# z weights ahead of the sums of blocks, low parts one sum behind, and a head's outputs sent from another tile, in a hybrid encoder layer on one Trainium2 core

## The chip, the cores and the metric

The kernel runs on one core of a Trainium2 chip. The metric is the device time of one execution in microseconds (us). Before the change the median of three runs is 2003.53 us.

## What is computed

One encoder layer over 1040 tokens (16 learned ones and 1024 of the input) of width 1024, all in float32. The part that matters here is the input projection and its users:

```python
proj = h @ w_in[l]
(q, k, v, z, b_raw, a_raw, sc_b, sc_c, sc_x, gate_a, gate_b) = jnp.split(proj, SPLIT_POINTS, axis=-1)
o_dn = gated_deltanet_bidir(q, k, v, z, b_raw, a_raw, conv_w, A_log, dt_bias, norm_w)  # ends in o * silu(z)
y_a = o_dn @ w_branch_dn[l]
y_b = (sc_b * depthwise_conv_centred(sc_c * sc_x, sc_conv_w[l])) @ w_branch_sc[l]
merged = jax.nn.sigmoid(gate_a) * y_a + jax.nn.sigmoid(gate_b) * y_b
h_res = h_res + merged @ w_out[l]
```

Then follow a SwiGLU block and a last normalisation. z has eight heads of 128 columns. gate_a and gate_b have eight column blocks of 128 each; block j of both is called pair j here.

## The kernel before

**Products in two parts.** A float32 operand is split into a high part, rounded to the type that TensorE (PE) takes in one pass, and a low part, the remainder: `split` (L100) lets ScalarE (ACT) copy the high part (L101) and VectorE (DVE) subtract it (L102). A product is then three matmuls per block of 128 rows: high by high, high by low, low by high. Weight blocks come by DMA into one of a few raw tiles and are split into tiles `wh` and `wl`, two slots each (`wtiles`, L111; `wload`, L117).

**Phase 1** (to about 970 us). Projections of all heads and of most other columns run on PE, and the scans of the eight heads lie between them, in an order that a planner writes out with estimated times. In `g_scan`, head h keeps its values in the tile `vS` (one buffer) and its decay matrices in `NP` (two buffers); the outputs replace parts of `NP`. At the end, for each half of the tokens, four transposes go to a bank, ACT copies the bank (L951) to a free part `oT` of `NP`, and a DMA stores it to `o_d[h]` (L953). The next head's values are written to `vS` by ACT (L808); the head after it writes `NP` by DVE (L639).

**The border** (from 970 us). The last three z-heads, 5, 6 and 7, and pairs 4 to 7 of the gates come after the scans. `z_rows(h)` runs z-head h in two halves of 24 matmuls (L134 to L136); ACT takes a tanh of the bank (L1493), DVE multiplies (L1495), and a DMA stores the result. The pairs use a scheme with seven block products in place of eight. It needs four sums of blocks of h, T1 to T4, each formed by DVE from large blocks (128x2048) and split in two parts. `moving_sums` (L1442) is a generator that forms one of them at each `next`: T1 in tiles mA, b3 and then b0; T2 in mA and b1; T3 in b3 and b2; T4 in mA and, after T3, b3. DVE's subtractions stand under L179, its additions under L1409, ACT's high parts under L101.

`pair(n, j, ...)` with n = j - 4 takes a bank of tag d (`pss`, three banks, in turn) and runs: A11 times B11 into it, ACT's copy of it (L1534), A12 times B21 into another bank, then S2 times T2 added into the first bank, S1 times T1, S3 times T3, S4 times B22 and A22 times T4, all at L1440. Pair 4's weights are prepared ahead, in three steps (`pair_weights`). z-head 7's two halves also use banks of tag d.

**What sets the order.** Phase 1 is written out for all engines. From L1484 to the end of pair 4, `border0` keeps DVE's and PE's instructions in the order of the code; ACT's and the queue's are placed by the scheduler, and so is all that comes after pair 4, which the scheduler may put between the instructions of the border. On each engine the built order is then fixed, and a waiting instruction holds those behind it.

Of the kernel before, what the change touches and what calls it, by code (L numbers as in the profile page):

```python
# [16 lines left out]
P = 128  # L17
# [7 lines left out]
H = 8  # L25
# [8 lines left out]
OQ, OK, OV, OZ, OBA, OSB, OSC, OSX, OGA, OGB = (  # L34
    0, 1024, 2048, 3072, 4096, 4128, 5152, 6176, 7200, 8224)


def unit(col):

    return (col if col < OBA else col - 32) // P  # L40
# [8 lines left out]
def encoder_layer(ctx: ExitStack, tc: tile.TileContext, x, meta, norm1_w, w_in, w_ba,  # L49
                  dn_conv_w, A_log, dt_bias, dn_norm_w, sc_conv_w, w_bdn, w_bsc,  # L50
                  w_out, norm2_w, w_gu, w_down, final_w, out):
    nc = tc.nc
# [12 lines left out]
    def uid(s):  # L65
        cnt["n"] += 1
        return f"{s}_{cnt['n']}"
# [29 lines left out]
    def transpose(dst, src, n=P):  # L97
        nc.tensor.transpose(dst, src, ident[:n, :n])

    def split(hi, lo, src):  # L100
        nc.scalar.copy(hi, src)  # L101
        nc.vector.tensor_tensor(out=lo, in0=src, in1=hi.bitcast(F32), op=ALU.subtract)  # L102
# [8 lines left out]
    def wtiles(shape):  # L111
        return [wp.tile(shape, F32R, tag=g, name=uid(g), bufs=2) for g in ("wh", "wl")]

    def staged(shape):
        return *wtiles(shape), rawtile(shape)

    def wload(src, j):  # L117
        wh, wl, raw = staged([P, KT, P])
        nc.sync.dma_start(raw, src[j])
        split(wh, wl, raw)  # L120
        return wh, wl
# [56 lines left out]
    def sub(out, a, b):  # L178
        nc.vector.tensor_tensor(out=out, in0=a, in1=b, op=ALU.subtract)  # L179
# [91 lines left out]
    def pe(ns):  # L271
        T["pe"] += ns
        return T["pe"] + HOP

    def V(n, kind=0):
        return on("dve", (68 + 1.042 * n, 130 + 1.042 * n, 130 + 0.52 * n)[kind])

    def A(n):
        return on("act", 144 + 0.834 * n)
# [505 lines left out]
    def g_scan(h, st_):  # L785
        nonlocal freed
        kq, vT, small, kn, NP, PQ, Pm = (st_[k] for k in ("kq", "vT", "small", "kn", "NP", "PQ", "Pm"))
# [4 lines left out]
        vS = dn.tile([P, 9, P], F32, tag="vS", name=uid("vS"))  # L792
        yield from take("scan")

        def newbank():
            return pss().rearrange("p (a n) -> p a n", a=4)
# [63 lines left out]
        for i in range(NC):  # L860
# [6 lines left out]
            t = pe(215 * len(act_))  # L867
# [5 lines left out]
            for d in act_:  # L873
# [4 lines left out]
                t = V(P, 1)  # L878
# [7 lines left out]
            for d in range(2):  # L886
# [3 lines left out]
                t = A(P)  # L890
# [5 lines left out]
            if i < NC - 1:  # L896
# [3 lines left out]
                t = pe(430)  # L900
# [3 lines left out]
            t2 = pe(430)  # L904
            if i < NC - 1:
                yield t
                for d in range(2):
# [6 lines left out]
                    t = V(P, 1)  # L914
# [28 lines left out]
            yield T["pe"] + 300  # L943
        yield T["dve"] + HOP
        for c4 in range(2):
            oT = NP[:, 4 * c4:4 * c4 + 4, 1 - c4]
            pt = newbank()
            for c in range(4):
                transpose(pt[:, c], oacc[4 * c4 + c])
            yield pe(430)  # L950
            nc.scalar.copy(oT, pt)  # L951
            A(512)
            nc.sync.dma_start(o_d[h][:, c4 * 512:(c4 + 1) * 512].rearrange("p (c t) -> p c t", c=4), oT)  # L953
# [82 lines left out]
    with tc.tile_pool(name="st", bufs=1) as st:  # L1036
# [64 lines left out]
        def high(t, g):  # L1101
            p = size(t)
            nc.scalar.copy(hx[0][:, 4 * g:4 * g + 4, C0 + P * t:C0 + P * t + p], banks[t, g][:, :, :p])  # L1103
# [297 lines left out]
    def big(tag, shape, dtype=F32R):  # L1401
        return tp.tile(shape, dtype, tag=tag, name=uid(tag))
# [9 lines left out]
    mov = {}  # L1412
# [29 lines left out]
    def moving_sums():  # L1442

        c = [slice(C0 + META + 512 * i, C0 + META + 512 * i + 512) for i in range(2)]
        f = lambda m: m.bitcast(F32)
        h0, h1 = ([f(hx[0][:, 4 * i:4 * i + 4, cc]) for cc in c] for i in range(2))
        l0, l1, l2 = ([f(t[:, :, cc]) for cc in c] for t in low_tiles)
        for i in range(2):
            for j in range(2):
                mov[f"B{i + 1}{j + 1}"] = hx[0][:, 4 * i:4 * i + 4, c[j]], [hx[1][4 * i + k][:, c[j]] for k in range(4)]  # L1450
        for i, n in enumerate(("T1", "T2", "T3")):
            t = big(f"b{i}", [P, 2, 4, 512])
            mov[n] = t[:, 0], t[:, 1]
        x, y = (big(g, [P, 2, 4, 512], F32) for g in ("mA", "b3"))
        t1, t2, t3, d_ = x[:, 0], x[:, 1], y[:, 0], y[:, 1]
        a, b = slice(0, 2), slice(2, 4)
        sub(t1, h0[1], h0[0])
        sub(d_, l0[1], l0[0])
        add(t1, t1, d_)
        split(*mov["T1"], t1)  # L1460
        yield
        sub(t2, h1[1], t1)
        add(t2[:, a], t2[:, a], l1[1])
        add(t2[:, b], t2[:, b], l2[1])
        split(*mov["T2"], t2)
        yield
        sub(t3, h1[1], h0[1])
        sub(d_[:, a], l1[1], l0[1][:, a])
        sub(d_[:, b], l2[1], l0[1][:, b])
        add(t3, t3, d_)  # L1470
        split(*mov["T3"], t3)
        yield
        t = big("b3", [P, 2, 4, 512])
        mov["T4"] = t[:, 0], t[:, 1]
        sub(t1, h1[0], t2)
        add(t1[:, a], t1[:, a], l1[0])
        add(t1[:, b], t1[:, b], l2[0])
        split(*mov["T4"], t1)
        yield

    raw_slots.extend((tp, f"raw{i}") for i in range(2))
    left, right = slice(0, 512), slice(512, 1024)
    border0 = ExitStack()
    border0.enter_context(tc.manual_schedule(engines={mybir.EngineType.DVE, mybir.EngineType.PE}))  # L1484
    z_units = [wload(w_in, unit(OZ + ZH * P))]

    def z_rows(h):
# [13 lines left out]
    def pair_weights(n, j):  # L1501

        s_hl[n % 2] = big(("mB", "mA")[n % 2], [P, 2, 2, KT, P])
        if n == 0:
            u = big("w2", [P, 2, 4, P])
            u_hl[0] = u[:, 0], u[:, 1]
        elif n == 1:
            u_hl[1] = [tp.tile([P, 4, P], F32R, tag="t2", name=uid("u_hl"), bufs=2) for _ in range(2)]
        gh, gl = wtiles([P, KT, P])
        rg, ru = (rawtile([P, KT, P]) for _ in range(2))  # L1510
        nc.sync.dma_start(rg, w_in[unit(OGA + j * P)])
        nc.sync.dma_start(ru, w_in[unit(OGB + j * P)])
        A_ = {"A11": (gh[:, 0:4], gl[:, 0:4]), "A12": (gh[:, 4:8], gl[:, 4:8])}

        def first():
            split(gh, gl, rg)

        def second():
            split(*u_hl[n % 2], ru[:, 4:8])
            A_["A22"] = u_hl[n % 2]  # L1520
            sums(rg, ru, rg[:, 0:4], rg[:, 4:8], ru[:, 0:4], ru[:, 4:8])
            stationary2(n, ru, rg, ru, A_)
        return A_, first, second

    def pair(n, j, A_, first, second):
# [54 lines left out]
        return o1  # L1580

    sums_of_blocks = moving_sums()
    z0, z1, z2 = (z_rows(h) for h in range(ZH, H))
    next(sums_of_blocks)
    z_units.append(wload(w_in, unit(OZ + (ZH + 1) * P)))
    next(z0)
    next(z0)
    next(sums_of_blocks)
    z_units.append(wload(w_in, unit(OZ + (H - 1) * P)))
    next(z0)  # L1590
    pair0 = pair_weights(0, GH)
    next(z1)
    pair0[1]()
    next(z1)
    pair0[2]()
    next(z1)
    next(z2)
    next(sums_of_blocks)
    next(z2)
    next(sums_of_blocks)  # L1600
    next(z2)
    for n, j in enumerate(range(GH, KT)):
        o1 = pair(n, j, *(pair_weights(n, j) if n else pair0))
        if n == 0:
            border0.close()
# [55 lines left out]
    mov = {n: (b_hl[:, 2 * i], b_hl[:, 2 * i + 1]) for i, n in enumerate(("B11", "B21"))}  # L1661
# [84 lines left out]
    t = KT - 1  # L1746
# [229 lines left out]
```

## Time and profile before

| | |
|---|---|
| runs | 2002.02, 2003.53, 2005.52 us |
| the profiled execution | 2004.27 us |
| its span, first to last instruction | 2002.5 us |
| PE busy | 1977.3 us, 99% of the span |
| DVE, ACT busy | 1396.6 us, 836.4 us |
| mean granted clock of PE | 0.995 |
| border, z-heads 5 to 7 on PE | 970.18 to 1009.33 us |

The profile is of one execution; what lies around its span is 2004.27 - 2002.5 = 1.77 us. Rows of a list in order of time read: start, duration, engine, line, operation, output <- inputs (names of tiles without numbers), shapes, and in brackets the idle time of the engine before it with what ended it. "pm", "pe" and "pd" are banks of the tags m, e and d. A table of stretches gives each engine's busy time with the number of its instructions, PE's granted clock (1.00 is full speed) and the DMA's share.

### The profile page before, as it was taken

To read this page: it belongs to the slowest core of one execution; us is meant where nothing else is said; L and a number is where in the kernel's file an instruction comes from. 1 tells how busy PE (TensorE), PEld (TensorE's weight loads), DVE (VectorE), ACT (ScalarE), POOL (GpSimd) and SP (SyncE) were. 2 spreads that over 40 slices of the span, in tenths; PEclk is the share of its full clock that TensorE was granted. 3 is DMA by queue.
4 is the path that set the end of the run, shared out by engine and by line. 5 is a ranking of instruction groups with operands and counts; after the bars stand their busy time and mean duration, and the time that the engine had idled before them with its cause. 6 is when DMAs were issued, how large, how long until landed. Compare 5 with 4: busy or idle time off the path is not lost.

```text
span 2002.5 us, 31873 instructions
## 1 busy us (share of the span) xinstructions
PE 1977.3 (99%) x12011; PEld 1724.1 (86%) x12011; DVE 1396.6 (70%) x3013; ACT 836.4 (42%) x1961; POOL 107.8 (5%) x407
## 2 busy tenths in 40 slices
PE   9999999999999999999999999999999999999998
PEld 8998889899999999999788888887878888888887
DVE  6887688878888888855685544469766666656575
ACT  6472465536463646333244221225323333334344
POOL 2011101010101010100000000000000000000000
PEclk9999999999999999999999999999999999999999
DMA  3123222222132222221236743123765345477654
GB/s 132 65 90 95 80 80 75 85 61 83 45 99 59 75 59 75 59 65 43 95 116 242 249 160 95 63 93 110 256 217 217 123 155 188 158 273 244 195 172 167
DMA packets 131121, 251.00 MB, mean 125 GB/s; under 512 B 45013, under 2 KB 54662, under 8 KB 128535
## 3 DMA queue, kind: packets, MB, share of 16 engines
q1 hardware_dynamic: 130391, 247.92, 37.5%
q8 instruction: 94, 1.54, 0.3%
q10 hardware_dynamic: 576, 1.05, 0.1%
q14 instruction: 60, 0.49, 0.1%
HBM read 180.67 MB, written 68.25 MB: 124 GB/s over the span
## 4 chain that ended last, share of the span: by engine, by line
PE 90%; DVE 4%; DMA 3%; ACT 1%; issue 1%; SPq 0%; DVEq 0%; ACTq 0%
PE pm L341 33%; PE pd L1440 12%; PE pe L1440 5%; PE pm L1440 3%; PE pd L903 1%; PE pd L882 1%; PE pd L866 1%; PE pe L136 1%; PE pe L134 1%; PE pd L869 1%; PE pe L135 1%; PE pe L603 1%; PE pd L134 1%; PE pd L136 1%; PE pd L135 1%; PE pe L1882 1%
## 5 line engine op out<-in xcount | busy, mean ns | idle before, releaser
L341 PE MATMUL pm<-hTh,wh 128*128 128x512 f32 (+4 forms) x1296 | 446.4, 350 | 0.3 <-ACT hTh L1103 0.2
L341 PE MATMUL pm<-al,wh 128*128 128x512 f32 (+4 forms) x1296 | 445.9, 349 | 0.0
L341 PE MATMUL pm<-hTh,wl 128*128 128x512 f32 (+4 forms) x1296 | 443.8, 348 | 0.0
L341 PEld LDWEIGHTS pm<-hTh,wh 128*128 128x128 f32 x1296 | 242.7, 188 | 13.7 <-issue 0.8
L341 PEld LDWEIGHTS pm<-hTh,wl 128*128 128x128 f32 x1296 | 242.9, 188 | 12.3 <-issue 0.4
L341 PEld LDWEIGHTS pm<-al,wh 128*128 128x128 f32 x1296 | 242.9, 188 | 12.2 <-issue 0.4
L102 DVE TENSOR_TENSOR al<-raw,ring_h 128x1024 fp32r<-128x1024 f32 x73 | 88.6, 1222 | 65.0 <-ACT ring_h L101 64.7
L101 ACT CAST ring_h<-raw 128x1024 fp32r<-128x1024 f32 x73 | 76.7, 1053 | 107.8 <-PE pd L1884 34.4
L990 DVE TENSOR_TENSOR wl<-raw,wh 128x512 fp32r<-128x512 f32 x118 | 79.5, 688 | 30.6 <-ACT wh L993 30.2
L363 DVE SCALAR_TENSOR_TENSOR kq<-ra,wc,kq 128x520 f32<-128x520 f32 x128 | 96.6, 755 | 4.8 <-ACT kq L393 3.5
L889 ACT ACTIVATE w<-pd,small 128x128 f32<-128x128 f32 x128 | 39.9, 363 | 117.1 <-PE pd L882 116.7
L101 ACT CAST wh<-raw 128x1024 fp32r<-128x1024 f32 x47 | 49.3, 1050 | 87.4 <-PE pe L135 25.5
L496 DVE TENSOR_TENSOR tm<-fP,fN 128x135 f32<-128x135 f32 (+23 forms) x248 | 72.0, 290 | 4.9
L500 DVE TENSOR_TENSOR fP<-fP,tm 128x135 f32<-128x135 f32 (+23 forms) x248 | 71.6, 289 | 5.1
L993 ACT CAST wh<-raw 128x512 fp32r<-128x512 f32 x118 | 69.2, 621 | 3.7 <-issue 3.6
L1409 DVE TENSOR_TENSOR b<-pd,b 128x512 f32<-128x512 f32 x22 | 15.2, 690 | 69.4 <-PE pd L1440 69.4
L1819 ACT ACTIVATE b<-b 128x512 f32<-128x512 f32 x22 | 13.9, 632 | 114.3 <-DVE b L1409 114.3
L102 DVE TENSOR_TENSOR wl<-raw,wh 128x1024 fp32r<-128x1024 f32 x47 | 57.3, 1219 | 3.8 <-ACT wh L101 3.7
L856 ACT ACTIVATE jk<-NP 128x128 f32<-128x128 f32 x64 | 19.9, 311 | 83.5 <-DVE NP L852 82.5
L876 DVE SCALAR_TENSOR_TENSOR r<-pd,negEG,vS 128x128 f32<-128x128 f32 x120 | 36.8, 345 | 25.7 <-PE pd L866 25.2
L1440 PE MATMUL pd<-b_hl,wh 128*128 128x512 f32 x176 | 54.5, 391 | 0.0
L912 DVE SCALAR_TENSOR_TENSOR S<-S,eGl,pd 128x128 f32<-128x128 f32 x104 | 31.6, 342 | 30.2 <-PE pd L899 29.8
(590 smaller groups left out, 4689.5 us busy)
## 6 DMA issues: line engine op xcount, KB each, us to landing
raw<-in_w_in_dram SPq DMA_DIRECT2D x72, 512.0 KB
raw<-in_w_gate_up_dram SPq DMA_DIRECT2D x44, 512.0 KB
sums<-in_w_down_dram SPq DMA_DIRECT2D x22, 512.0 KB
t_d<-sums SPq DMA_DIRECT2D x11, 1024.0 KB
raw<-s_d SPq DMA_DIRECT2D x44, 256.0 KB
raw<-t_d SPq DMA_DIRECT2D x44, 256.0 KB
act_d<-b SPq DMA_DIRECT2D x43, 256.0 KB
raw<-act_d SPq DMA_DIRECT2D x33, 256.0 KB
```

Source lines behind the costliest of these rows:

```text
L101: nc.scalar.copy(hi, src)
L102: nc.vector.tensor_tensor(out=lo, in0=src, in1=hi.bitcast(F32), op=ALU.subtract)
L134: mm(po[:m, :n], wh[:, k, :m], xhk[:, t0:t0 + n], start=(k == 0), stop=False)
L135: mm(po[:m, :n], wh[:, k, :m], xlk[:, t0:t0 + n], start=False, stop=False)
L136: mm(po[:m, :n], wl[:, k, :m], xhk[:, t0:t0 + n], start=False, stop=(k == KT - 1))
L341: mm(po[:, :n], ww[:, k], f(k)[:, t0:t0 + n], start=i == 0, stop=i == 3 * KT - 1)
L363: nc.vector.scalar_tensor_tensor(out=acc, in0=raw[:, h0 + t:h0 + t + hn], scalar=wc[:, t, col:col + 1], in1=acc, op0=ALU.mult, op1=ALU.add)
L496: nc.vector.tensor_tensor(out=tv, in0=fP[:, 0:r, j:j + 1].broadcast_to([P, r, n]), in1=fN[:, j:j + 1, j + 1:32].broadcast_to([P, r, n]), o ...
L500: nc.vector.tensor_tensor(out=fP[:, 0:r, j + 1:32], in0=fP[:, 0:r, j + 1:32], in1=tv, op=ALU.subtract)
L990: nc.vector.tensor_tensor(out=u[1][1][:, k], in0=u[2][:, k], in1=u[1][0][:, k].bitcast(F32), op=ALU.subtract)
L993: nc.scalar.copy(u[1][0][:, k], u[2][:, k])
L1440: mm(po, x[:, k], y, start=k + i == 0 and not add_to, stop=k == 3 and i == 2, skip_group_check=add_to)
```

## The change

The outputs of a head go by way of `vS` in place of `NP`. `moving_sums` gives out a high part in one step and its low part in the next, with the next sum's DVE work between them, so that it has more steps. z-head 6's weights are loaded and split ahead of T1, z-head 7's after T2's high part. ACT joins DVE and PE in `border0`.

```diff
@@ g_scan
-            oT = NP[:, 4 * c4:4 * c4 + 4, 1 - c4]
+            oT = vS[:, 4 * c4:4 * c4 + 4]
@@ moving_sums
+        high = lambda n, t: nc.scalar.copy(mov[n][0], t)
+        low_part = lambda n, t: sub(mov[n][1], t, f(mov[n][0]))
         sub(t1, h0[1], h0[0])
         sub(d_, l0[1], l0[0])
         add(t1, t1, d_)
-        split(*mov["T1"], t1)
+        high("T1", t1)
         yield
         sub(t2, h1[1], t1)
         add(t2[:, a], t2[:, a], l1[1])
         add(t2[:, b], t2[:, b], l2[1])
-        split(*mov["T2"], t2)
+        high("T2", t2)
+        low_part("T1", t1)
+        yield
+        low_part("T2", t2)
         yield
         sub(t3, h1[1], h0[1])
         sub(d_[:, a], l1[1], l0[1][:, a])
         sub(d_[:, b], l2[1], l0[1][:, b])
         add(t3, t3, d_)
-        split(*mov["T3"], t3)
+        high("T3", t3)
+        yield
+        sub(t1, h1[0], t2)
+        low_part("T3", t3)
         yield
         t = big("b3", [P, 2, 4, 512])
         mov["T4"] = t[:, 0], t[:, 1]
-        sub(t1, h1[0], t2)
         add(t1[:, a], t1[:, a], l1[0])
         add(t1[:, b], t1[:, b], l2[0])
-        split(*mov["T4"], t1)
+        high("T4", t1)
+        yield
+        low_part("T4", t1)
         yield
@@ the border
-    border0.enter_context(tc.manual_schedule(engines={mybir.EngineType.DVE, mybir.EngineType.PE}))
+    border0.enter_context(tc.manual_schedule(engines={mybir.EngineType.DVE, mybir.EngineType.PE, mybir.EngineType.Activation}))
...
-    next(sums_of_blocks)
     z_units.append(wload(w_in, unit(OZ + (ZH + 1) * P)))
     next(z0)
+    next(sums_of_blocks)
+    next(sums_of_blocks)
     next(z0)
+    z_units.append(wload(w_in, unit(OZ + (H - 1) * P)))
     next(sums_of_blocks)
-    z_units.append(wload(w_in, unit(OZ + (H - 1) * P)))
     next(z0)
+    next(z1)
     pair0 = pair_weights(0, GH)
     next(z1)
     pair0[1]()
     next(z1)
     pair0[2]()
-    next(z1)
     next(z2)
     next(sums_of_blocks)
     next(z2)
     next(sums_of_blocks)
+    next(sums_of_blocks)
     next(z2)
+    next(sums_of_blocks)
```

In the built order tile names carry numbers that differ between the two programs. DVE at the start of the border, before the change (wl_12346 is the low part of z-head 6's weights, b_2088_12335 T1's low part):

```order
L179 TENSOR_TENSOR mA_12338<-hTh 128x2048
L179 TENSOR_TENSOR b_2092_12339<-al_124 128x2048
L1409 TENSOR_TENSOR mA_12338<-mA_12338,b_2092_12339 128x2048
L102 TENSOR_TENSOR b_2088_12335<-mA_12338,b_2088_12335 128x2048
L102 TENSOR_TENSOR wl_12346<-raw_12347,wh_12345 128x1024
```

The same place now (wl_12336 is z-head 6's, b_2093_12368 T1's low part):

```order
L102 TENSOR_TENSOR wl_12336<-raw_12337,wh_12335 128x1024
L179 TENSOR_TENSOR mA_12371<-hTh 128x2048
L179 TENSOR_TENSOR b_2097_12372<-al_124 128x2048
L1409 TENSOR_TENSOR mA_12371<-mA_12371,b_2097_12372 128x2048
L179 TENSOR_TENSOR mA_12371<-hTh,mA_12371 128x2048
L1409 TENSOR_TENSOR mA_12371<-mA_12371,al_125 128x1024
L1409 TENSOR_TENSOR mA_12371<-mA_12371,al_126 128x1024
L179 TENSOR_TENSOR b_2093_12368<-mA_12371,b_2093_12368 128x2048
```

The weights have moved ahead of T1, and T1's low part behind the forming of T2.

PE after pair 4's second product, before the change (pm_12578 is that product's bank, pd_12564 pair 4's bank of tag d, mB_12418 holds its S blocks, b_2089_12336 is T2; twelve matmuls each):

```order
L1440 MATMUL pm_12578<-al_126,wh_12420 128x512
L1440 MATMUL pm_12578<-hTh,wl_12421 128x512
L1440 MATMUL pd_12564<-b_2089_12336,mB_12418 128x512 x12
L1440 MATMUL pe_12593<-b_2088_12335,mB_12418 128x512 x12
L1440 MATMUL pd_12564<-b_2090_12337,mB_12418 128x512
```

The same place now. pd_12675 is pair 5's bank and pd_12795 pair 6's; pair 5's three rows shown are the last of twelve matmuls, A11 times B11:

```order
L1440 MATMUL pm_12578<-al_126,wh_12447 128x512
L1440 MATMUL pm_12578<-hTh,wl_12448 128x512
...
L1440 MATMUL pd_12675<-hTh,wh_12667 128x512
L1440 MATMUL pd_12675<-al_124,wh_12667 128x512
L1440 MATMUL pd_12675<-hTh,wl_12668 128x512
L1440 MATMUL pd_12795<-hTh,wh_12787 128x512
L1440 MATMUL pd_12795<-al_124,wh_12787 128x512
L1440 MATMUL pd_12564<-b_2094_12369,mB_12445 128x512 x12
L1440 MATMUL pe_12593<-b_2093_12368,mB_12445 128x512 x12
```

Fourteen matmuls of pairs 5 and 6 now stand ahead of pair 4's third product. In the order before the change, pair 5's twelve come behind pair 4's S4 times B22.

DVE now, from pair 4's last S block to the operation on z-head 7's second half (pd_12495 and pd_12527 are the banks of z-head 7's halves; b_2097_12372 is where T3 is formed, mA_12371 T4, b_2095_12370 T3's low part):

```order
L102 TENSOR_TENSOR mB_12445<-raw_12450,mB_12445 128x1024
L179 TENSOR_TENSOR b_2097_12372<-hTh 128x2048
L179 TENSOR_TENSOR b_2097_12372<-al_125,al_124 128x1024
L179 TENSOR_TENSOR b_2097_12372<-al_126,al_124 128x1024
L102 TENSOR_TENSOR wl_12668<-raw_12669,wh_12667 128x1024
L1409 TENSOR_TENSOR b_2097_12372<-b_2097_12372 128x2048
L1504 TENSOR_SCALAR s_2111_12494<-s_2111_12494,pd_12495 128x512
L179 TENSOR_TENSOR mA_12371<-hTh,mA_12371 128x2048
L179 TENSOR_TENSOR b_2095_12370<-b_2097_12372,b_2095_12370 128x2048
L1409 TENSOR_TENSOR mA_12371<-mA_12371,al_125 128x1024
L1409 TENSOR_TENSOR mA_12371<-mA_12371,al_126 128x1024
L1504 TENSOR_SCALAR s_2111_12494<-s_2111_12494,pd_12527 128x512
```

Before, the order was T3's forming, T3's low part, the operation on the first half, T4's forming, T4's low part, the operation on the second half. T3's low part has moved behind the first operation, into the forming of T4, and T4's low part behind the second. On ACT the copy of pair 4's bank (L1534, now L1543) stood directly behind the tanh of z-head 7's second half; now it is here (b_2114_12555 is T4's high part):

```order
L1457 COPY b_2095_12370<-b_2097_12372 128x2048
L1502 ACTIVATE s_2111_12494<-pd_12527 128x512
L1457 COPY b_2114_12555<-mA_12371 128x2048
L1543 COPY s_2115_12562<-pd_12564 128x512
```

T4's high part now stands ahead of that copy.

## The prediction

> **What bounds the kernel now.** I read the page first, for the shares of the engines and the chain that ended last; then the idle time of PE with its releasers; then, around the one stall that the diff touches, the instructions of DVE, ACT and PE in order of time, and a table of short stretches with the granted clock.
>
> ```profile
> PE 1977.3 (99%) x12011; PEld 1724.1 (86%) x12011; DVE 1396.6 (70%) x3013; ACT 836.4 (42%) x1961; POOL 107.8 (5%) x407
> PE 90%; DVE 4%; DMA 3%; ACT 1%; issue 1%; SPq 0%; DVEq 0%; ACTq 0%
> ```
>
> PE is busy 99% of the span and carries 90% of the chain. A change that leaves PE's work as it is can only take away PE's idle time, or its time at a low clock, or add to them. The work is untouched here: every matmul of before is in the changed program.
>
> ```profile
> 970.18 0.39 PE L134 MATMUL pm<-hTh,wh 128*128 128x512 f32 x1
> ...
> 981.29 0.39 PE L135 MATMUL pe<-al,wh 128*128 128x512 f32 x1
> 985.51 0.79 PE L136 MATMUL pe<-hTh,wl 128*128 128x512 f32 x1 [3.83 <-DVE wl L102]
> ...
> 998.45 0.39 PE L134 MATMUL pd<-hTh,wh 128*128 128x512 f32 x1
> ...
> 1014.77 2.88 PE L1440 MATMUL pd<-b,mB 128*128 128x512 f32 x12
> ...
> 1028.14 0.39 PE L1440 MATMUL pd<-hTh,wh 128*128 128x512 f32 x1
> ```
>
> These are PE's rows at the border between the heads' phase and the pairs. The z-heads 5, 6 and 7 run from 970.18, 48 matmuls each. The 50th matmul starts at 981.29, so one takes (981.29 - 970.18) / 49 = 0.2267 us. The third matmul of z-head 6 then waits 3.83 us for DVE's low part of its weights. At 1014.77 pair 4 starts its third product, S2 times T2.
>
> ```profile
> core 0: us, PE busy (x) PEld busy (x) DVE busy (x) ACT busy (x) POOL busy (x), PEclk, DMA share, GB/s
> 981.70:985.50 3.80, 0.00 (x0) 0.00 (x0) 3.47 (x3) 1.72 (x3) 0.00 (x0) 0.78 0.00 0
> 985.50:990.60 5.10, 5.09 (x12) 4.03 (x13) 5.07 (x4) 0.00 (x0) 0.00 (x0) 0.50 0.31 103
> 990.60:1000.00 9.40, 9.40 (x42) 7.79 (x42) 4.52 (x5) 4.04 (x4) 0.00 (x0) 1.00 0.29 81
> 1492.60:1494.60 2.00, 0.02 (x1) 0.00 (x0) 1.97 (x4) 0.00 (x0) 0.00 (x0) 1.00 0.00 0
> 1495.80:1499.20 3.40, 3.40 (x10) 2.66 (x9) 0.69 (x1) 0.40 (x2) 0.00 (x0) 0.50 0.78 284
> ```
>
> The stall costs more than its 3.83 us: the clock is 0.50 until 990.60, and 12 matmuls take 5.10 us there, 0.425 us each. Even an idle time of 2.0 us, at 1492.60, was followed by 3.4 us at 0.50.
>
> **Term A, the stall that goes.** Why was the low part late?
>
> ```profile
> 970.15 1.05 ACT L101 CAST wh<-raw 128x1024 fp32r<-128x1024 f32 x1 [9.82 <-PE pm L341]
> 980.09 1.91 ACT L101 CAST b<-mA 128x2048 fp32r<-128x2048 f32 x1 [3.67 <-DVE mA L1409]
> 998.47 1.05 ACT L101 CAST wh<-raw 128x1024 fp32r<-128x1024 f32 x1 [4.66 <-PE pe L135]
> 999.42 0.58 ACT L1493 ACTIVATE s<-pe 128x512 f32<-128x512 f32 x1
> 1012.25 0.59 ACT L1534 COPY s<-pd 128x512 f32<-128x512 f32 x1 [1.36 <-PE pd L1440]
> ```
>
> ```profile
> 970.38 0.69 DVE L451 TENSOR_TENSOR rb<-pm,rb 128x512 f32<-128x512 f32 x1 [4.70 <-PE pm L341]
> 973.24 2.29 DVE L179 TENSOR_TENSOR mA<-hTh 128x2048 f32<-128x2048 f32 x1 [2.16 <-DMA p_d<-rb]
> 975.45 2.28 DVE L179 TENSOR_TENSOR b<-al 128x2048 f32<-128x2048 f32 x1
> 977.76 2.29 DVE L1409 TENSOR_TENSOR mA<-mA,b 128x2048 f32<-128x2048 f32 x1
> 982.03 2.29 DVE L102 TENSOR_TENSOR b<-mA,b 128x2048 fp32r<-128x2048 f32 x1 [1.98 <-ACT b L101]
> 984.24 1.22 DVE L102 TENSOR_TENSOR wl<-raw,wh 128x1024 fp32r<-128x1024 f32 x1
> ...
> 999.55 1.23 DVE L102 TENSOR_TENSOR wl<-raw,wh 128x1024 fp32r<-128x1024 f32 x1 [2.90 <-ACT wh L101]
> ...
> 1007.43 2.36 DVE L102 TENSOR_TENSOR mB<-raw,mB 128x1024 fp32r<-128x1024 f32 x2 [1.12 <-ACT mB L101]
> 1009.71 0.68 DVE L1495 SCALAR_TENSOR_TENSOR s<-s,pe 128x512 f32<-128x512 f32 x1
> 1010.31 2.28 DVE L179 TENSOR_TENSOR b<-hTh 128x2048 f32<-128x2048 f32 x1
> ...
> 1015.91 2.28 DVE L1409 TENSOR_TENSOR b<-b 128x2048 f32<-128x2048 f32 x1
> ...
> 1022.66 0.68 DVE L1495 SCALAR_TENSOR_TENSOR s<-s,pd 128x512 f32<-128x512 f32 x1
> 1023.26 2.28 DVE L179 TENSOR_TENSOR mA<-hTh,mA 128x2048 f32<-128x2048 f32 x1
> 1025.58 2.36 DVE L1409 TENSOR_TENSOR mA<-mA,al 128x1024 f32<-128x1024 f32 x2
> ```
>
> The high part of z-head 6's weights was there at 970.15 + 1.05 = 971.2, but the low part stood on DVE behind all of T1, and T1's low part waited for ACT. Now it stands in front: DVE is free at 971.07, so it is done at 971.2 + 1.22 = 972.4, before T1 can start (973.24, when the transfer out of the memory under mA has ended), and 9 us before PE asks for it. The cover is those 9 us. So A = -(3.83 + 12 x (0.425 - 0.2267)) = **-6.2 us**.
>
> Z-head 7's weights take the slot of z-head 5, free at 970.18 + 48 x 0.2267 = 981.06. ACT now does both high parts first. T1 ends on DVE at 980.05, T2's subtraction and two additions (2.28 + 2.36) end about 984.6, T2's high part at 986.5, a tanh and the cast (0.58 + 1.05) at 988.1, and after 1.22 us of DVE the low part at 989.4. PE asks at 970.18 + 98 x 0.2267 = 992.4. That is hidden with 3 us to spare, and T1's and T2's low parts (2.29 each) lie beside z-heads 6 and 7.
>
> **Term B, what is late next.** Without the stall PE ends z-head 6 at 970.18 + 96 x 0.2267 = 991.94, z-head 7 at 1002.83, and pair 4's first two products at 1008.27. By then both parts of T2 are ready, but pair 4's third product is no longer next in PE's queue: the built order puts twelve matmuls of pair 5's first product and two of pair 6's in front of it. Banks of tag d are three, taken in turn: z-head 7's two halves and pair 4 hold them, so pair 5's request gets the bank of z-head 7's first half and pair 6's that of its second. DVE's operation on that half (L1495, now L1504) must have read it first. DVE has that operation behind the forming of T3, and the one on the second half behind T3's low part and the forming of T4. In before, pair 5's product started at 1028.14, after the operation of 1022.66: no wait. PE does not pass a waiting matmul (at 981.29 the matmuls behind the waiting one had their data, and none ran).
>
> When does DVE get there? Pair 4's weights need z-head 6's slot, so DVE's chain hangs on the end of z-head 6. In before, from that end (998.45) to T3's first operation (1010.31) it took 11.86 us. The chain now has one operation of 0.60 us less on DVE, and one tanh of 0.58 us more ahead of it on ACT: 991.94 + 11.86 = 1003.8. T3's formation takes 1015.91 + 2.28 - 1010.31 = 7.88 us, the operation on the bank 0.6 more: **1012.3**. PE idles 4.0 us. Then T4's subtraction, T3's low part, two additions and the operation on the second half: 2.28 + 2.29 + 2.36 + 0.68, less 0.3 for starts that overlap (973.24 to 975.45 is 2.21), 7.3 us: **1019.6**. Pair 5's twelve matmuls are long done by then, at either clock.
>
> Next comes the third product, which adds to pair 4's bank and so waits for ACT's copy of it (L1534, now L1543). With ACT's order now written out too, that copy stands behind T4's high part. In before the copy ran at 1012.25, 16 us ahead of T4. T4's high part starts when the additions are done, about 1019.0, takes 1.91, and the copy 0.59: **1021.5**.
>
> So from 1008.27 to 1021.5, 13.2 us, PE issues 14 matmuls, worth 14 x 0.2267 = 3.2 us. B = **+10.1 us**. Behind the two waiting products stands all of PE's work; nothing of it gets through.
>
> **Term C, the clock.** No row shows this pattern of idle times (4.0, then 2 to 5, then 1.5 us, with 14 matmuls between). Nearest are the 5.10 us (12 matmuls, 2.4 us lost) and the 3.4 us after 1495.80. Bounds: 0, if the clock is back when the third product starts, and 2.4. I take one stretch of 3.4 us at half speed, 8 matmuls at 0.425: 8 x 0.2 = **+1.6 us**, as the last idle time before it is the short one.
>
> The Trainium skill ("TensorE: Matmul & The Clock Gate", section "Why this matters for your kernels") says that PE gaps up to about 3 us keep the clock, and that an idle window of about 3.4 us halves it. The trace disagrees: 2.0 us sufficed at 1492.60. By the page the short idle times at the end would cost nothing and C would be 0.
>
> **Term D, the heads' outputs.** The copy and the two transfers keep their place in all queues, only the tile differs. What it moves are two waits for the transfer.
>
> ```profile
> 375.80 0.38 SPq L953 DMA_DIRECT2D o_d<-NP  x1
> 382.64 0.61 DVE L639 SCALAR_TENSOR_TENSOR NP<-pe,small,PQ 128x128 f32<-128x128 f32 x2 [1.41 <-DMA o_d<-NP]
> 883.07 1.28 SPq L953 DMA_DIRECT2D o_d<-NP  x2
> 892.85 0.86 ACT L808 ACTIVATE vS<-pd,small 16x128 f32<-16x128 f32 x3 [1.50 <-PE pd L98]
> ```
>
> Once NP was held 1.41 us by a transfer that landed 6.8 us after its issue; that wait goes, though PE shows no idle time there. In its place the next head's values wait for the same transfer, as vS has one buffer. The shortest distance is the last head's, 884.35 to 892.85, 8.5 us, against 6.8 us for the slowest landing: covered by 1.7 us. I take 0, with -1.4 and +1 as ends; the scan behind ACT would pay if the cover went.
>
> **Sum.** The profiled execution took 2004.27 us (span 2002.5, and 1.77 around it): 2004.27 - 6.2 + 10.1 + 1.6 = **2009.8 us**. The median shown is 2003.53, 0.7 below, within the spread of the three runs (2002.02 to 2005.52). Past pair 4 the orders soon agree again and DVE and ACT have slack, so I let the shift stand to the end.
>
> **Rivals.**
> 1. Faster: the stall goes and nothing takes its place, 2004.27 - 6.2 = 1998.1. It needs DVE and ACT to reach pair 4's copy early. The full gain needs the copy done by 1008.27 + 3.2 = 1011.4; the point of no change is 1014.77 + 14 x 0.2267 = 1017.9, where before had issued as many matmuls. For it: DVE's chain holds idle times of 2.90 and 1.12 us. Against: the first was mostly PE's own work on z-head 6, and without both the copy still ends at 1017.5. Chance 0.05.
> 2. The clock is full again at the third product (the page's rule, and the lower end of C): 2008.2. For it, 14 matmuls run between the waits; against, 2.0 us of idleness was enough. Chance 0.14.
> 3. The edits give a little back, D's 1.4 us and 1 to 2 us of DVE's idle times: 2005 to 2007.5. Chance 0.09.
> 4. The low clock lasts for two stretches, or DVE's backlog stops PE once more within pair 4: 2011.8 to 2013. T4's low part ends near 1024 and is needed at 1032, which speaks against. Chance 0.08.
>
> That the edit doesn't do what it says is excluded by the built order: the weights do stand in front. My forecast, 2008.5 to 2011.5, has 0.64.
>
> **How the numbers follow.** A measurement of this kernel tells about 0.2% from no change, 4.0 us: 1999.5 to 2007.5. Faster is rival 1, 0.05. Within is rival 3 and the low edge of rival 2, 0.11. Slower is the rest, 0.84. The range leaves out rival 1, part of rival 3 and the upper half of rival 4: 2006.5 to 2012.6.
>
> **What would show it.** Right, if PE has no idle time before 1008, z-head 6 ends near 992, and then three idle times follow: about 4 us before pair 5's first product, released by DVE's operation on z-head 7; 2 to 5 us before pair 6's two matmuls, by the same line; and 1 to 2 us before S2 times T2, by ACT's copy; with a clock of 0.5 around them. T3's first operation should start near 1004 and the copy end near 1021.5. Wrong, if pair 5's product starts by 1010, if the copy on ACT runs before T4's high part, or if vS waits for a DMA.

## The result, and the profile after

The changed kernel takes **2009.22 us**, median of 8 runs (2006.81 to 2010.51). The kernel before takes 2003.55 us beside it, median of 8 runs (2001.18 to 2006.41). The ratio is 1.0028, 95% interval 1.0019 to 1.0037: slower by 0.28%. The profiled execution took 2007.99 us, with a span of 2006.3 us.

From the page after, the engines' busy time and the shares of the chain that ended last:

```profile
PE 1978.7 (99%) x12011; PEld 1724.6 (86%) x12011; DVE 1396.7 (70%) x3013; ACT 836.3 (42%) x1961; POOL 107.4 (5%) x407
PE 89%; DVE 5%; DMA 2%; ACT 2%; issue 1%; SPq 0%; DVEq 0%; ACTq 0%
```

The counts of instructions are those of before. PE's share of the chain is down from 90% to 89% and DVE's up from 4% to 5%: a per cent is 20 us, too coarse for this difference, so the rows at the border have to tell.

PE's rows at the border after, in order of time (start, duration, instruction; in brackets the idle time ahead of it and what released it):

```profile
1002.68 0.39 PE L1440 MATMUL pd<-hTh,wh 128*128 128x512 f32 x1
...
1007.89 0.39 PE L1440 MATMUL pm<-hTh,wl 128*128 128x512 f32 x1
1012.36 0.77 PE L1440 MATMUL pd<-hTh,wh 128*128 128x512 f32 x1 [4.08 <-DVE s L1504]
...
1017.19 0.63 PE L1440 MATMUL pd<-hTh,wl 128*128 128x512 f32 x1
1019.54 0.50 PE L1440 MATMUL pd<-hTh,wh 128*128 128x512 f32 x1 [1.72 <-DVE s L1504]
1019.88 0.40 PE L1440 MATMUL pd<-al,wh 128*128 128x512 f32 x1
1021.47 4.47 PE L1440 MATMUL pd<-b,mB 128*128 128x512 f32 x12 [1.18 <-issue]
1025.78 2.89 PE L1440 MATMUL pe<-b,mB 128*128 128x512 f32 x12
```

The 3.83 us stall of z-head 6 is gone, and pair 4 starts at 1002.68 where it would have with no idle time at all. But pair 4's third product, S2 times T2, starts at 1021.47. In before it started at 1014.77. Three new idle times stand in front of it: 4.08 us, released by DVE's operation on the first bank of z-head 7; 1.72 us, by the same line for the second bank; and 1.18 us for which the profile names nothing. The rows of DVE and ACT name it:

```profile
1003.72 2.28 DVE L179 TENSOR_TENSOR b<-hTh 128x2048 f32<-128x2048 f32 x1
...
1011.53 0.68 DVE L1504 SCALAR_TENSOR_TENSOR s<-s,pd 128x512 f32<-128x512 f32 x1
...
1018.81 0.68 DVE L1504 SCALAR_TENSOR_TENSOR s<-s,pd 128x512 f32<-128x512 f32 x1
```

```profile
992.00 0.60 ACT L1502 ACTIVATE s<-pe 128x512 f32<-128x512 f32 x1 [3.49 <-PE pe L136]
...
1011.65 1.90 ACT L1457 CAST b<-b 128x2048 fp32r<-128x2048 f32 x1 [2.47 <-DVE b L1409]
...
1018.98 1.91 ACT L1457 CAST b<-mA 128x2048 fp32r<-128x2048 f32 x1 [4.93 <-DVE mA L1409]
1020.79 0.57 ACT L1543 COPY s<-pd 128x512 f32<-128x512 f32 x1
```

ACT idles 4.93 us ahead of T4's high part (1018.98), and pair 4's copy stands behind it although the copy's data have been there since pair 4's first product, that is since about 1005.6. The copy ends at 1020.79 + 0.57 = 1021.36, and S2 times T2 starts 0.11 us later.

A table of short stretches of after, cut where the granted clock changes and each 3.41 us long, shows the clock (busy time and number of instructions of each engine, then the granted clock):

```profile
core 0: us, PE busy (x) PEld busy (x) DVE busy (x) ACT busy (x) POOL busy (x), PEclk, DMA share, GB/s
1010.96:1014.38 3.42, 2.02 (x5) 1.66 (x6) 3.42 (x4) 2.40 (x2) 0.00 (x0) 0.50 0.00 0
1014.38:1017.79 3.41, 3.41 (x9) 2.14 (x7) 3.41 (x4) 0.00 (x0) 0.00 (x0) 0.50 0.00 0
1017.79:1021.20 3.41, 0.77 (x3) 0.30 (x2) 3.41 (x5) 2.22 (x2) 0.00 (x0) 1.00 0.26 105
1021.20:1024.61 3.41, 3.14 (x8) 2.50 (x9) 3.41 (x5) 1.31 (x3) 0.00 (x0) 0.50 0.14 54
```

The clock is at 0.50 from 1010.96 to 1017.79 and from 1021.20 to 1024.61. The first of the two costs nothing: it slows the twelve matmuls of pair 5, which end before the second bank is free. The second slows S2 times T2: 1025.78 - 1021.47 = 4.31 us for twelve matmuls instead of 2.72.

**Where the time went.** S2 times T2 starts 1021.47 - 1014.77 = 6.7 us later than before, with 14 matmuls (3.2 us) already done that came behind it in before: +3.5 us. The low clock in it adds 4.31 - 2.72 = 1.6, together +5.1 us at the border. The profiled executions differ by less in the end, 2007.99 - 2004.27 = 3.7 us. Far behind the border, near 1385 us, the same matmul starts 4.8 us later than in before (1390.09 against 1385.32), 0.3 less than this sum; a low clock that lasts longer there adds 0.9. Then one stall gives more than that back, first in before, then in after:

```profile
1494.67 4.55 PE L1440 MATMUL pd<-b,w 128*128 128x512 f32 x12 [2.05 <-DVE b L1409]
```

```profile
1500.19 3.02 PE L1440 MATMUL pd<-b,w 128*128 128x512 f32 x12 [1.75 <-DVE b L1409]
```

The idle time ahead of it is 0.3 us shorter after, and the twelve matmuls behind it ran at full clock, 3.02 us instead of 4.55: 1.8 us won back. These are single executions; the medians of 8 runs each differ by 5.7 us.

### The profile page after: what moved, and what is told of

Its sections match the earlier page's. It is cut to its first block, busy times and chain, and to the rows that moved or that the text cites. A ratio compares the mean times of both kernels' runs of the same rounds, so it can differ in the third digit from the quotient of the medians.

```text
span 2006.3 us, 31885 instructions
## 1 busy us (share of the span) xinstructions
PE 1978.7 (99%) x12011; PEld 1724.6 (86%) x12011; DVE 1396.7 (70%) x3013; ACT 836.3 (42%) x1961; POOL 107.4 (5%) x407
## 3 DMA queue, kind: packets, MB, share of 16 engines
q8 instruction: 94, 1.54, 0.3%
## 4 chain that ended last, share of the span: by engine, by line
PE 89%; DVE 5%; DMA 2%; ACT 2%; issue 1%; SPq 0%; DVEq 0%; ACTq 0%
PE pm L341 33%; PE pd L1440 12%; PE pe L1440 5%; PE pm L1440 3%; PE pd L903 1%; PE pd L882 1%; PE pd L866 1%; PE pe L136 1%; PE pe L135 1%; PE pe L134 1%; PE pd L869 1%; PE pe L603 1%; PE pe L1896 1%; PE pe L1894 1%; PE pe L1895 1%; PE pd L899 1%
## 5 line engine op out<-in xcount | busy, mean ns | idle before, releaser
L101 ACT CAST ring_h<-raw 128x1024 fp32r<-128x1024 f32 x73 | 76.7, 1054 | 107.4 <-PE pe L1896 35.5
L101 ACT CAST wh<-raw 128x1024 fp32r<-128x1024 f32 x47 | 49.4, 1050 | 85.1 <-PE pe L135 20.9
```

## The experiments

My theory was: the change gains what it says at z-head 6 and pays for it with what ACT's written-out order puts ahead of pair 4's copy. With the copy late, the built order lets matmuls of pairs 5 and 6 go ahead of S2 times T2, and those wait for z-head 7's banks on DVE. The rivals: the outputs' tile costs; the two banks alone are the loss; the low parts or the operations on z-head 7, late on DVE, are the loss whatever ACT does. Each kernel was timed in five rounds beside the kernel before.

### The heads' outputs alone

The kernel before with one line changed:

```
-            oT = NP[:, 4 * c4:4 * c4 + 4, 1 - c4]
+            oT = vS[:, 4 * c4:4 * c4 + 4]
```

> The kernel before with one edit: the heads' outputs go through the tile of their values (vS instead of NP), all else as it was. My theory (the loss of the change comes from pair 4's copy and z-head 7's two operations standing late in the written orders of ACT and DVE; the outputs' tile is worth nothing, term D = 0): 2003.5 us, the time of before, between 2002.1 (the 1.4 us wait of NP gained) and 2004.5. Rival (the outputs sent from vS hold up the heads, and that is a good part of the loss of 5.7 us): 2006 us or more, with DVE or ACT instructions that wait for the transfer out of vS.

Measured: 2002.81 us (2001.05 to 2005.41); before 2003.4; ratio 0.9999, interval 0.9990 to 1.0008. No difference. DVE's row at that place, to be set beside the one that waited 1.41 us in before:

```profile
381.31 0.59 DVE L639 SCALAR_TENSOR_TENSOR NP<-pe,small,PQ 128x128 f32<-128x128 f32 x2
```

It starts at 381.31 without a wait, where before started at 382.64. The wait is gone, DVE runs 1.3 us ahead there, and the time is the same: PE was not waiting for it.

### The new order, with the outputs put back

The changed kernel with that line as in before.

> The changed kernel with that same edit undone: outputs through NP again, the new order at the border kept. My theory: 2009.2 us, the time of the changed kernel, with the three idle times of PE at the border (4.1 us before pair 5's first product, 1.7 us before pair 6's two matmuls, 1.2 us before S2 times T2) all there. Rival (outputs): 2006 us or less, since the tile is put back.

Measured: 2010.77 us (2008.07 to 2012.1), ratio to before 1.0034, interval 1.0022 to 1.0045. PE's waits at the border in this kernel (engine, line, what it waited for; total, times, longest):

```profile
PE pd L1440 <- DVE s L1504: 5.9, 2, 4.1
PE pd L1440 <- issue: 1.2, 1, 1.2
```

The same three idle times, and a time whose range overlaps that of the changed kernel. With the first experiment this takes the outputs out of the account: the whole loss is the border's.

### ACT's order left free

```
-    border0.enter_context(tc.manual_schedule(engines={mybir.EngineType.DVE, mybir.EngineType.PE, mybir.EngineType.Activation}))
+    border0.enter_context(tc.manual_schedule(engines={mybir.EngineType.DVE, mybir.EngineType.PE}))
```

> The changed kernel with ACT taken out of the written-out order at the border, as it was before; the z weights in front, the low parts one sum behind, and DVE's and PE's written orders stay. In the built order ACT then does the copy of pair 4's bank ahead of the high part of T3, and PE does S2 times T2 and S1 times T1 (24 matmuls) before any matmul of pair 5. My theory: the copy needs only pair 4's first product, which ends near 1005.5 us in the changed kernel's trace, so it is done by about 1007, before PE ends the second product at 1008.2; S2 times T2 starts without a wait, none of the three idle times is left, and the clock stays full there. Of the sum only term A remains: 2003.5 - 6.2 = 1997.3 us (1996 to 1999). Rival 1 (it is DVE's operations on z-head 7, written behind T3 and T4, that cost, wherever the copy stands): PE still waits about 4 us for the first bank, and the time stays at 2006 to 2009 us. Rival 2 (the moved low parts of T1 to T4 are themselves late for pair 4's products): S2 times T2 or S1 times T1 waits for DVE, 2000 to 2004 us.

Measured: **1995.94 us** (1995.25 to 1999.97), ratio to before 0.9965, interval 0.9952 to 0.9977; the median lies just below the expected 1996 to 1999. ACT's and PE's rows, and a table of two stretches:

```profile
1005.71 0.59 ACT L1543 COPY s<-pd 128x512 f32<-128x512 f32 x1 [1.36 <-PE pd L1440]
...
1011.10 1.92 ACT L1457 CAST b<-b 128x2048 fp32r<-128x2048 f32 x1 [1.80 <-DVE b L1409]
```

```profile
1008.23 2.88 PE L1440 MATMUL pd<-b,mB 128*128 128x512 f32 x12
1010.95 2.88 PE L1440 MATMUL pe<-b,mB 128*128 128x512 f32 x12
```

```profile
core 0: us, PE busy (x) PEld busy (x) DVE busy (x) ACT busy (x) POOL busy (x), PEclk, DMA share, GB/s
970.00:1008.20 38.20, 38.20 (x170) 31.66 (x169) 34.73 (x30) 14.88 (x17) 0.00 (x0) 1.00 0.33 118
1008.20:1024.00 15.80, 15.80 (x71) 12.86 (x70) 15.80 (x14) 7.64 (x8) 0.00 (x0) 1.00 0.08 33
```

The copy runs at 1005.71, as soon as the product is there, and T3's high part (1011.10) behind it. S2 times T2 starts at 1008.23 instead of 1021.47. PE has no idle time in 54 us, at full clock. DVE's operations on z-head 7 are hardly earlier than in the changed kernel: the second starts at 1018.25 here, and nobody waits for it. So neither the low parts one sum behind nor DVE's order is the loss by itself. One word in the list of engines is 13 us. It leaves all of ACT's order to the scheduler, though; that it is the copy's place in it is the matter of the last three experiments.

### The z weights moved, and nothing else

The kernel before, with each of two lines moved over one other:

```
-    next(sums_of_blocks)
     z_units.append(wload(w_in, unit(OZ + (ZH + 1) * P)))
+    next(sums_of_blocks)
     next(z0)
     next(z0)
-    next(sums_of_blocks)
     z_units.append(wload(w_in, unit(OZ + (H - 1) * P)))
+    next(sums_of_blocks)
     next(z0)
```

> The kernel before with only the two orders of z weights moved: z-head 6's weights ahead of T1, z-head 7's ahead of T2. Each sum keeps its low part right behind its high part, ACT is not written out, pair 4's steps and the outputs stay as in before. My theory: both low parts of weights are on DVE early enough, z-head 6 does not stall, and nothing else is late: term A alone, 2003.5 - 6.2 = 1997.3 us (1996 to 1999). Rival (without the low parts moved one sum behind, z-head 7's weights stand behind T1's whole split and come late, which is why the change moved the low parts too): a stall of 2 to 3 us at the third matmul of z-head 7, clock loss with it, 2000 to 2003 us.

Measured: 1996.71 us (1996.26 to 1999.04), ratio to before 0.9968, interval 0.9956 to 0.9981. DVE's two low parts of z weights in this kernel:

```profile
970.99 1.22 DVE L102 TENSOR_TENSOR wl<-raw,wh 128x1024 fp32r<-128x1024 f32 x1 [0.17 <-ACT wh L101]
...
984.58 1.22 DVE L102 TENSOR_TENSOR wl<-raw,wh 128x1024 fp32r<-128x1024 f32 x1
```

Both are done before PE asks (about 981.5 and 992.4 by the steps of the prediction), though T1's low part still stands right behind its high part. The rival falls: the low parts one sum behind are not needed to hide z-head 7's weights. This and the kernel with ACT left free, whose ranges overlap, are the two fastest of all.

### Z-head 6's weights alone

The kernel before with the first of these two moves only.

> The kernel before with z-head 6's weights alone moved ahead of T1; z-head 7's stay behind T2, all else as before. My theory: the 3.83 us stall goes, and z-head 7's weights are the next that come late: they stand on DVE behind T1's low part and all of T2, which ended in before about 997, and PE, without the stall, asks for them at 992.4. A stall of 2 to 3 us at z-head 7 with half a clock stretch behind it: 2001 to 2002.5 us, a gain of 1 to 2.5 us. Rival (the slots and ACT give z-head 7 enough time by themselves, so moving one head's weights is the whole gain): 1997 us and no stall.

Measured: 2002.0 us (1999.85 to 2003.59), ratio 0.9990, interval 0.9982 to 0.9999.

```profile
995.27 0.60 PE L136 MATMUL pd<-hTh,wl 128*128 128x512 f32 x1 [2.42 <-DVE wl L102]
995.66 0.63 PE L134 MATMUL pd<-hTh,wh 128*128 128x512 f32 x1
...
998.23 0.63 PE L134 MATMUL pd<-hTh,wh 128*128 128x512 f32 x1
```

The stall has moved one head on, 2.42 us, and the matmuls behind it are 0.43 us apart from 995.66 to 998.65. Most of the gain is lost: the two moves are worth 6.7 us together and 1.4 us with the second left out.

### The banks alone

The changed kernel, z-head 7's operations written ahead of T3, pair 4's copy still behind T4's high part:

```
     next(z2)
-    next(sums_of_blocks)
+    next(z2)
     next(z2)
     next(sums_of_blocks)
     next(sums_of_blocks)
-    next(z2)
+    next(sums_of_blocks)
     next(sums_of_blocks)
```

> The changed kernel with z-head 7's two operations on DVE (and the second tanh on ACT) moved ahead of T3 in the written order; T3 and T4 as a whole follow, and pair 4's copy still stands behind T4's high part on ACT. The banks of z-head 7 come free by about 1005 us instead of 1012.2 and 1019.4. My theory: it only moves the wait. The copy ends after T4's high part as before (1021.4 us in the changed kernel's trace), the built order still has 13 matmuls of pairs 5 and 6 ahead of S2 times T2, and the low parts of those pairs' weights now stand behind the same DVE chain; S2 times T2 starts at 1021 to 1023 us again, and the time stays at 2009.2 us (2008 to 2011). Rival (the two bank waits of 4.1 and 1.7 us are the loss, the copy's 1.2 us only a rest of it): the 5.8 us of idle time and some 1.6 us of low clock go, 2002 to 2004 us.

Measured: 2009.56 us (2009.18 to 2011.92), ratio to before 1.0032, interval 1.0019 to 1.0044.

```profile
1009.59 0.50 PE L1440 MATMUL pd<-hTh,wh 128*128 128x512 f32 x1 [0.78 <-ACT wh L101]
1010.75 0.50 PE L1440 MATMUL pd<-hTh,wl 128*128 128x512 f32 x1 [0.43 <-DVE wl L102]
1021.36 0.79 PE L1440 MATMUL pd<-hTh,wl 128*128 128x512 f32 x1 [8.05 <-DVE wl L102]
1022.14 4.70 PE L1440 MATMUL pd<-b,mB 128*128 128x512 f32 x12
```

```profile
1019.66 1.90 ACT L1457 CAST b<-mA 128x2048 fp32r<-128x2048 f32 x1 [4.83 <-DVE mA L1409]
1021.47 0.58 ACT L1543 COPY s<-pd 128x512 f32<-128x512 f32 x1
```

No wait for a bank is left, and nothing is won. Fifteen matmuls of pairs 5 and 6 stand ahead of S2 times T2 here (the expectation said 13). The last of them, pair 6's third, waits 8.05 us for the low part of its weights, which DVE makes behind T4's additions; then S2 times T2 starts at 1022.14, right after the copy (1021.47 + 0.58 = 1022.05). So the banks are not the loss. What the idle time is put down to changes with DVE's order. This run alone does not tell which of the two set the end of the wait, the low part (1020.09 + 1.22 = 1021.31) or the copy, as they end within 0.8 us of each other; the last experiment does.

### T4's high part behind the copy

The changed kernel; T4's high and low part are written inside pair 4, T3's high part stays ahead:

```
         add(t1[:, b], t1[:, b], l2[0])
+        yield
         high("T4", t1)
...
             nc.scalar.copy(o1[:, left], bank)
+            if n == 0:
+                for _ in range(2):
+                    next(sums_of_blocks)
...
     next(z2)
-    next(sums_of_blocks)
     for n, j in enumerate(range(GH, KT)):
```

> The changed kernel with T4's high part (and the low part, which needs it) written behind pair 4's copy on ACT; T4's additions and z-head 7's operations on DVE stay where they are, and T3's high part stays ahead of the copy. My theory: T3's high part ends at 1013.5 us (1011.65 + 1.90), the tanh 0.5 later, so the copy is done at 1014.6 instead of 1021.4. In the built order twelve matmuls of pair 5 still stand ahead of S2 times T2, the two of pair 6 no longer. So PE waits 4.1 us for the first bank as before, does the twelve until about 1015 to 1017.5, and goes on with S2 times T2 with at most 0.5 us of wait: it starts 4 to 6 us earlier than the 1021.5 of the changed kernel, and the time is 2004 us (2003 to 2006). Rival (the place of the copy decides nothing, PE would have waited for the second bank anyway): 2008 us or more.

Measured: 2003.67 us (2001.53 to 2007.3), ratio to before 1.0003, interval 0.9994 to 1.0012.

```profile
1012.53 0.47 PE L1440 MATMUL pd<-hTh,wh 128*128 128x512 f32 x1 [4.08 <-DVE s L1505]
...
1014.79 5.46 PE L1440 MATMUL pd<-b,mB 128*128 128x512 f32 x12 [0.60 <-issue]
```

```profile
1014.12 0.58 ACT L1544 COPY s<-pd 128x512 f32<-128x512 f32 x1
```

The copy ends at 1014.70, S2 times T2 starts at 1014.79, 6.7 us earlier than in the changed kernel. The built order now has five matmuls of pair 5 in front of it, not twelve as the expectation said; the 4.08 us for the first bank are all there. The time is that of before: of the 13.3 us between the changed kernel and the one with ACT left free, 5.6 are back. Of the 6.7 us that S2 times T2 starts earlier, about 3 are lost again: nine matmuls fewer are done before it (9 x 0.2267 = 2.0 us), and at the low clock its twelve take 1020.05 - 1014.79 = 5.26 us instead of the 4.31 of the changed kernel.

### The copy ahead of both high parts

The changed kernel, ACT written out as there, but with T3's and T4's high parts (and, for the data's sake, the steps that hang on them) written behind the copy. DVE's order up to T4's forming stays:

```
         add(t3, t3, d_)
-        high("T3", t3)
         yield
+        high("T3", t3)
         sub(t1, h1[0], t2)
...
             nc.scalar.copy(o1[:, left], bank)
+            if n == 0:
+                next(sums_of_blocks)
+                next(sums_of_blocks)
+                next(z2)
+                next(sums_of_blocks)
...
     next(z2)
-    next(sums_of_blocks)
-    next(sums_of_blocks)
-    next(z2)
-    next(sums_of_blocks)
     for n, j in enumerate(range(GH, KT)):
```

> The changed kernel with pair 4's copy ahead of the high parts of T3 and T4 in ACT's written order, ACT still written out, and DVE's order as in the changed kernel up to T4's forming (T4's low part falls behind one addition of pair 4). z-head 7's operations on DVE stay behind T3 and T4. My theory: the copy is done at about 1006.3 us, S2 times T2 and S1 times T1 follow pair 4's first two products without a wait and cover 5.4 us of DVE's work, so the first bank (free at 1012.2) is not waited for; at the second bank (free at 1019.4) or at the weights of pair 6 PE may wait once or twice, 1 to 2 us in all. Of the loss over a version with term A alone (2009.2 - 1996 = 13 us) nine tenths go: 1998 to 2001 us. Rival (what stands late on DVE, T3, T4 and z-head 7's operations, limits the start of pair 5 whatever ACT does): 2004 to 2009 us.

Measured: 1998.89 us (1996.52 to 2004.06), ratio to before 0.9980, interval 0.9970 to 0.9989.

```profile
1008.50 2.88 PE L1440 MATMUL pd<-b,mB 128*128 128x512 f32 x12
1011.22 2.88 PE L1440 MATMUL pe<-b,mB 128*128 128x512 f32 x12
1021.65 0.50 PE L1440 MATMUL pd<-hTh,wl 128*128 128x512 f32 x1 [1.00 <-DVE wl L102]
```

```profile
1011.91 0.68 DVE L1504 SCALAR_TENSOR_TENSOR s<-s,pd 128x512 f32<-128x512 f32 x1
...
1019.18 0.68 DVE L1504 SCALAR_TENSOR_TENSOR s<-s,pd 128x512 f32<-128x512 f32 x1
```

DVE's operations on z-head 7 are as late as in the changed kernel, 1011.91 and 1019.18, and the waits for them are gone: S2 times T2 and S1 times T1 (24 matmuls, 5.4 us) run from 1008.50 in the place of the 14 that waited. One idle time of 1.00 us is left. Moving the copy ahead of the two high parts (with the order of PE that the scheduler builds on it) is worth 10.3 us against the changed kernel's median. The rival, that DVE limits the start of pair 5 whatever ACT does, falls.

## Why the prediction was right, point by point

**A, the stall that goes (-6.2 us): right.** PE has no idle time at z-head 6 or 7, the tanh that waits for z-head 6's end starts at 992.00 (forecast for that end: 991.94), pair 4 starts at 1002.68 (forecast 1002.83). Where A stands alone, with the z weights moved and nothing else, the time falls by 2003.40 - 1996.71 = 6.7 us. That z-head 7's weights would be the next to come late was right as well: left in place, they cost 2.42 us and a stretch of low clock. The size of the term is a little short. By the starts of pair 4 the stall was worth 1009.33 - 1002.68 = 6.65 us, and the forecast's own start, 1002.83, already gives 6.5. The 3.83 us in brackets count from the modelled end of the matmul ahead, 0.39 us after its start, while matmuls start 0.2267 us apart.

**B, what is late next (+10.1 us): right, waits and times, but for one length.** T3's first operation starts at 1003.72 (forecast 1003.8), the first bank is waited for until 1012.36 (1012.3), the second until 1019.54 (1019.6), S2 times T2 starts at 1021.47 (1021.5). The idle time ahead of the second bank is 1.72 us, shorter than the 2 to 5 that the forecast named, because the low clock stretched the twelve matmuls in front of it over 1012.36 to 1017.6; as the forecast said, that clock costs nothing there. What the forecast did not weigh is how the three waits hang together. It put them one behind another, as if each had its own price. The experiments show one cause: with the banks free early nothing is won (2009.56); with the copy early, and the banks as late as ever, 2009.22 - 1998.89 = 10.3 us are won, of the 13.3 that lie between the changed kernel and the one with ACT left free. The expectation's nine tenths were too many; its range of 1998 to 2001 us held.

**C, the clock (+1.6 us): right in size, in part by luck.** One stretch of 3.4 us at 0.50 lies in S2 times T2, 1.6 us. The reason given, that the last idle time is a short one, does not decide how long a low stretch lasts; the last section shows what goes with it. By the rule of the Trainium skill ("TensorE: Matmul & The Clock Gate", section "Why this matters for your kernels"), that PE gaps up to about 3 us keep the clock, the 1.72 and 1.18 us ahead of it would have cost nothing. The trace disagrees, and rival 2 falls with it.

**D, the heads' outputs (0): right.** Measured alone, the ratio is 0.9999 (0.9990 to 1.0008), and no engine waits for a transfer out of `vS`.

**Sum.** Forecast 2009.8, measured 2009.22. The border's terms, -6.2 + 10.1 + 1.6 = 5.5 us, compare with 5.1 us in the rows at the border (with 6.65 for A the terms give 5.1 as well) and 5.7 us between the medians. I let the shift stand to the end; the profiled execution lost 0.9 us near 1390 and won 1.8 back at the stall near 1500, which no term of the forecast held. That the sum comes within 0.6 us of the median is therefore in part luck: A is 0.4 short, and the forecast started from an execution 0.7 above before's median.

The profiles allow a comparison without these later stalls. Some 360 us behind the border one matmul waits 2.6 us for the same release (line L101 on ACT) in every kernel. Its start against that in before, beside the medians (up to 0.3 us of the difference is there before the border):

| kernel | start of that matmul | against before | median against before |
|---|---|---|---|
| before | 1385.32 us | | |
| after | 1390.09 | +4.8 | +5.7 |
| outputs alone | 1385.41 | +0.1 | -0.6 |
| outputs put back | 1390.05 | +4.7 | +7.4 |
| ACT left free | 1378.60 | -6.7 | -7.5 |
| z weights moved alone | 1378.49 | -6.8 | -6.7 |
| z-head 6's weights alone | 1383.36 | -2.0 | -1.4 |
| banks alone | 1391.13 | +5.8 | +6.1 |
| T4's high part behind the copy | 1386.56 | +1.2 | +0.2 |
| copy ahead of both high parts | 1380.27 | -5.1 | -4.5 |

The medians follow the border within about 1 us, but for the outputs put back: its median lies 2.7 us above, and its profile is of the fastest of its six runs. With ACT left free and with the z weights moved alone the border is worth the same, so the low parts one sum behind show no gain there. In the profile of the kernel with ACT left free the stall near 1500 is

```profile
1487.58 3.06 PE L1440 MATMUL pd<-b,w 128*128 128x512 f32 x12 [0.54 <-DVE b L1409]
```

0.54 us of idle time and no low clock, so part of what its median gains beyond the border lies there.

**Rival 1** (nothing takes the stall's place, 1998.1) is what the edit yields once the copy is ahead: 1995.94 us with ACT left free, 1998.89 with ACT written out. Its condition fits as well. It asked for the copy by 1011.4, and with ACT free the copy is done at 1005.71 + 0.59 = 1006.3. Its point of no change, 1017.9, was worked out for 14 matmuls ahead of S2 times T2. With T4's high part behind the copy there are five, which puts it at 1014.77 + 5 x 0.2267 = 1015.9; S2 times T2 started at 1014.79, 1.1 us ahead of that, and gave more than this back at the low clock: S1 times T1 follows at 1020.05, so the twelve matmuls of S2 times T2 took 5.26 us instead of 2.72.

```profile
1020.05 3.06 PE L1440 MATMUL pe<-b,mB 128*128 128x512 f32 x12
```

**Rivals 3 and 4** did not come. T3's first operation starts as late as forecast, so DVE gave nothing back; the third product has one low stretch, and PE does not wait again within pair 4.

## What to carry to other kernels

When an engine's order is written out by hand, every small instruction on it that PE waits for counts, not only the ones being placed: ask of each what it waits for, what stands ahead of it that waits longer, and who needs it. A wait that a trace puts down to one releaser can be the symptom of another: here PE waited at banks only because the product that should have filled the time was held by a 0.57 us copy on ACT. Look for what would have run in the gap, before making the named releaser faster.

## What the runs showed of the hardware

In these profiles PE's granted clock is 1.00 or 0.50, and within a run it changes only at times that are whole multiples of 3.41 us apart: in after at 1010.96, 1017.79, 1021.20 and 1024.61. What goes with a fall is how long PE was busy in such a step of 3.41 us, and not the length of an idle time. A single idle time of 2.35 us stands in two kernels, ahead of 1491.42 and of 1489.91. With the copy ahead it is split between two steps (the first two rows), and the clock stays at 1.00. With the z weights moved alone it lies in one step (the third row), and the next step is at 0.50 (PE's busy time is the second figure of a row, the clock the third from the end):

```profile
1486.88:1490.29 3.41, 2.19 (x10) 1.49 (x8) 1.61 (x3) 0.00 (x0) 0.00 (x0) 1.00 0.14 59
1490.29:1493.70 3.41, 2.28 (x10) 1.91 (x11) 2.36 (x4) 0.63 (x1) 0.00 (x0) 1.00 0.65 269
...
1488.02:1491.43 3.41, 1.52 (x7) 1.25 (x8) 2.68 (x5) 0.63 (x1) 0.00 (x0) 1.00 0.44 180
1491.43:1494.84 3.41, 3.41 (x10) 2.64 (x9) 1.05 (x3) 0.62 (x1) 0.00 (x0) 0.50 0.69 246
```

So it is in all ten profiles of this case, from 12 us on: the clock fell after every full-speed step in which PE was busy for up to 1.54 us, 35 in all, and after none with 1.55 or more. That is why 2.05 us of idle time cost a low stretch in before (1494.67), and 1.72 and 1.18 us with two matmuls between them did in the changed kernel (0.77 us busy in 1017.79 to 1021.20), while 1.75 us (1500.19) in the changed kernel did not.

The clock can also fall after PE has resumed, as it falls at the end of the step. In the kernel with T4's high part behind the copy PE started again at 1012.53, and a matmul took 0.40 us at 1013.07 and 0.63 us at 1013.56; the step ended at 1013.51.

A low stretch ends when PE was busy for nearly all of a step. The clock came back after every low step with 3.14 us or more and after none with up to 2.84; between the two, 2.88 brought it back, and 2.92, 3.00 and 3.08 did not. So the changed kernel's first low stretch lasted two steps (2.02 us busy in the first of them, from 1010.96) and its second only one (3.14 us busy from 1021.20). What decides between 2.84 and 3.14 us stays open.
